# Other buffers for the weights of a second matrix product, and more for its left sides

## The chip, the cores and the metric

The kernel runs on one core of a Trainium2 chip. Its engines are TensorE (PE in the rows: matmuls, with its weight loads as PEld), VectorE (DVE), ScalarE (ACT), GpSimd (POOL) and SyncE (SP), which issues nearly all DMA transfers here. Each engine carries out its own list of instructions in order; so does SyncE, and a transfer that has to wait for a buffer holds up every transfer behind it in that list. The metric is the time of one execution in microseconds of device time, less is better. The time of a kernel is the median of several runs.

## The reference

One layer of a transformer-like block on x of 1024 x 1024 float32: a mixer (sparse attention and a gated delta rule), then an MLP of 4096 hidden columns with a squared ReLU. The change is in the MLP's second product.

```python
x = x + rms_norm(mix, post_norm_mix[l])
h = rms_norm(x, pre_norm_mlp[l])
y = jnp.square(jax.nn.relu(h @ w_mlp_in[l])) @ w_mlp_out[l]
x = x + rms_norm(y, post_norm_mlp[l])
```

## The kernel before, in words

A float32 matrix product is made of three matmuls at TensorE's fast 32-bit format (`mm3`, lines 199 to 201): each operand is split by `parts` into a rounded high part (a ScalarE cast, line 1422) and the rest (a VectorE subtraction, line 1423).

The hidden columns are 32 blocks of 128. Four of them (`NS`, "plain") are multiplied in the ordinary way. The other 28 go as 14 pairs i = 0 to 13 (`NP2`) through a scheme of Strassen's kind with 7 products j = 1 to 7 instead of 8; its left sides are sums of quarters of the hidden activations, its right sides sums of quarters of the weights. In the first product the seven combinations of each pair's hidden values are made by VectorE and ScalarE (lines 1593 to 1620) and written to DRAM (`spill`, lines 1560 to 1566: tensors `hid`). The second product takes the pairs in chunks, (0, 1), then (2, 3, 4) to (11, 12, 13), and in each chunk the products in the order j = 1, 2, 5, 3, 6, 7, 4. For each (chunk, j), `both_parts` loads the left sides: for j = 1, 2, 4 they lie in DRAM in two parts already and come straight into `hq` (`hl` for the first ones, line 1656), for the other j they come as one block into a `tmp` buffer (line 1659) and are split. The right sides come from `raw`, the 256 x 1024 block of w_mlp_out of pair i (1 MB, `raw_out`, line 1645); for some j a VectorE sum into `tt` stands in between (lines 1665 to 1677). TensorE adds up four banks per j, and VectorE takes each bank into `acc` or `acc_u` (`gather`: a copy the first time, line 1707; an addition after that, line 1704), after which the bank is free for a later j. The first banks that are taken so are those of j = 1 of the first chunk, and j = 2 adds on in the same banks.

At the end come the plain rows: `plain` is loaded into `stg` and split into `hq` (lines 1734 to 1736), their rows of w_mlp_out are loaded (line 1738) and split, and for each of the 8 row blocks `tb` TensorE computes two banks (`sc`, `ch`), VectorE adds them to `acc` (line 1763), and `finish` makes the norm, loads x (line 1745) into one of the two `stg` buffers, updates it (line 1751) and stores it (line 1753).

Buffers are rings: the pool `raw` (2 buffers of 8 KB a partition) is that of w_mlp_in in the first product and takes i = 0 and 1 after it; `raw2` (5 of 8 KB) takes i from 2 on; `hq` has 12 of 2 KB, `tmp2` 17 of 2 KB, `stg` 2 of 4 KB. The pools `hq`, `raw2` and `tt` open in `room()`, when the right sides of the first product are done with. A scheduler orders all instructions ahead of time for each engine from the program, so the order in which transfers stand in SyncE's list is not that of the source.

Of the kernel before, what the change touches and what calls it, by code (L numbers as in the profile page):

```python
# [8 lines left out]
F32 = mybir.dt.float32  # L9
F32R = mybir.dt.float32r  # L10
# [8 lines left out]
P = 128  # L19
T = 1024  # L20
D = 1024
# [118 lines left out]
def block_kernel(ctx: ExitStack, tc: tile.TileContext, x, w_in, c_norm, w_uk, w_uv, rel_bias, conv_w, a_log,  # L140
                 dt_bias, o_norm, w_out, pre_norm_mix, post_norm_mix, pre_norm_mlp, post_norm_mlp,
                 w_mlp_in, w_mlp_out, out, dbg=None):
    nc = tc.nc
    dbg = dbg or {}
    V, S, G, PE, SY = nc.vector, nc.scalar, nc.gpsimd, nc.tensor, nc.sync
    pl = Pools(tc)
# [4 lines left out]
    dt_bias, o_norm, w_out, w_mlp_in, w_mlp_out = dt_bias[0], o_norm[0], w_out[0], w_mlp_in[0], w_mlp_out[0]  # L151
# [12 lines left out]
    const, _ = pl.open("const")  # L164
    ps_t, _ = pl.open("ps_t", bufs=2, space=PSUM)
    ps_c, _ = pl.open("ps_c", bufs=2, space=PSUM)
    ps_w, ps_w_close = pl.open("ps_w", bufs=2, space=PSUM)
    dram, _ = pl.open("dram", space=DRAM)
# [82 lines left out]
    stg, stg_close = pl.open("stg", bufs=2)  # L251
# [56 lines left out]
    for tb in range(NB):  # L308
        xt = pl.t(px, [P, D], F32, f"x{tb}")
        r0 = tb // 4 * 512 + tb % 2 * 256 + tb % 4 // 2  # L310
# [13 lines left out]
    for half in range(2):  # L324
# [9 lines left out]
        for k in range(NK):  # L334
# [3 lines left out]
            sl = slice(half * 512, half * 512 + 512)  # L338
# [686 lines left out]
    ps_a, _ = pl.open("ps_a", bufs=2, space=PSUM)  # L1025
    ps_s, _ = pl.open("ps_s", bufs=2, space=PSUM)
# [221 lines left out]
    pool, wo, h2, early = {}, [], {}, []  # L1248
# [168 lines left out]
    def parts(src, eng, pool=None, tag="hl"):  # L1417

        hi = pl.t(pool or hlp, [P, 512], F32R, tag)
        lo = pl.t(pool or hlp, [P, 512], F32R, tag)  # L1420
        h_, l_ = (t.rearrange("p (a b) -> p a b", a=src.shape[1]) if len(src.shape) == 3 else t for t in (hi, lo))
        S.copy(h_, src)  # L1422
        eng.tensor_sub(l_, src, h_.bitcast(F32))  # L1423
        return hi, lo
# [35 lines left out]
    def tmp(dtype=F32):  # L1460
        return pl.t(tmpp, [P, 512], dtype, "tmp2")
# [168 lines left out]
    def room():  # L1630

        if rooms:
            return
        tq_close()
        h2_close()
        rooms["acc"], _ = pl.open("yacc")
        rooms["hq"], _ = pl.open("hq", bufs=12)
        rooms["raw"], _ = pl.open("raw2", bufs=5)
        rooms["tt"], _ = pl.open("tt", bufs=6)

    def raw_out(i, pool):

        raw = pl.t(pool, [P, 2, D], F32, "raw")
        r0 = (NS + 2 * i) * P
        SY.dma_start(raw, w_mlp_out[r0:r0 + 256, :].rearrange("(a p) d -> p a d", p=P))
        return raw

    def both_parts(c, j, raws, ts):

        res = []  # L1650
        for i in chunks[c]:
            own = (hlp, "hl") if c == 0 and j == 1 else (rooms["hq"], "hq")
            if WHICH[j] < 3:
                h = tuple(pl.t(own[0], [P, 512], F32R, own[1]) for _ in range(2))
                for a in range(2):
                    SY.dma_start(h[a].bitcast(F32), hid_d[i, WHICH[j]][:, a])
            else:
                f = tmp()
                SY.dma_start(f, hid_d[i, WHICH[j]])
                h = parts(f, V, *own)  # L1660
            raw = raws[i]
            b11, b12, b21, b22 = raw[:, 0, LO], raw[:, 0, HI], raw[:, 1, LO], raw[:, 1, HI]
            if j == 5:
                t = ts[i] = pl.t(rooms["tt"], [P, 512], F32, "tt")
                V.tensor_sub(t, b12, b11)
            elif j == 6:
                t = ts[i]
                V.tensor_sub(t, b22, t)
            elif j == 4:
                t = ts[i]  # L1670
                V.tensor_sub(t, b21, t)
            elif j == 7:
                t = pl.t(rooms["tt"], [P, 512], F32, "tt")
                V.tensor_sub(t, b22, b12)
            else:
                t = {1: b11, 2: b21, 3: b22}[j]
            res.append((h, parts(t, V)))
        return res

    def sides():  # L1680
        raws, ts = {}, {}
        for i in chunks[0]:
            raws[i] = raw_out(i, rawp)
        for c, ch in enumerate(chunks):
            for j in ORDER:
                if j in (3, 6) and c + 1 < len(chunks):
                    i = chunks[c + 1][(3, 6).index(j)]
                    raws[i] = raw_out(i, rooms["raw"])
                if (c, j) == (0, 2):
                    room()  # L1690
                yield c, j, both_parts(c, j, raws, ts)
            if c + 1 < len(chunks):
                raws[chunks[c + 1][2]] = raw_out(chunks[c + 1][2], rooms["raw"])

    gen = sides()
    ready = [next(gen)]
# [32 lines left out]
    fin, _ = pl.open("fin")  # L1729
    rows = []  # L1730
    for f in range(NS):
        hq = pl.t(rooms["raw"], [P, 2, T], F32R, "raw")
        r = pl.t(stg, [P, T], F32, "stg")
        SY.dma_start(r, plain_d[f])
        S.copy(hq[:, 0], r)
        V.tensor_sub(hq[:, 1], r, hq[:, 0].bitcast(F32))
        raw = pl.t(rawp, [P, D], F32, "raw")
        SY.dma_start(raw, w_mlp_out[f * P:(f + 1) * P, :])
        rows.append((hq, [parts(raw[:, sl], V, *((hlp, "hl") if f < 2 else (rooms["hq"], "hq"))) for sl in (LO, HI)]))
    def finish(tb, yt):  # L1740
        xr = pl.t(stg, [P, D], F32, "stg")

# [50 lines left out]
```

## Time and profile before

| | us |
|---|---|
| median of 3 runs | 1416.54 |
| fastest and slowest of them | 1414.64, 1420.17 |
| the profiled execution, its time | 1417.32 |
| its span, first to last instruction | 1415.6 |
| busy in it: PE, DVE, ACT, POOL | 1299.8, 1104.6, 730.1, 272.0 |

The rows further on come from the one profiled execution; their times count from the span's start. Its mean granted TensorE clock is 0.950 of full speed. The second MLP product's first transfers start near 1059 us, the plain rows' part near 1355 us. Matmuls overlap, so a matmul's row can be longer than its step: the step is read from the starts of successive rows, or from the count in a stretch that is busy throughout.

### The profile page before, as it was taken

Reading aid. Unit: us, or ns where it says so; the run is one execution under the profiler, and the core shown is the slowest. Engines: PE = TensorE matmul, PEld = TensorE weight load, DVE = VectorE, ACT = ScalarE, POOL = GpSimd, SP = SyncE. Lnnn points to the kernel's source line nnn. Section 1 sums busy time; section 2 is a strip of 40 time slices with the busy share of each in tenths; the row PEclk is TensorE's granted clock in tenths of the full one; section 3 lists DMA queues with packets and bytes.
Section 4 is the critical chain, followed back from the end, with each engine's and each line's share of the span. In section 5 each row is a group of like instructions: output and inputs, shape, how many; then the busy total and the mean of one; then the engine's idle time right before and its main releaser. Section 6 shows DMA issues by size and latency. Waiting matters only on the chain. (4 is left out here: it accounts for less than half of the span.)

```text
span 1415.6 us, 20269 instructions
## 1 busy us (share of the span) xinstructions
PE 1299.8 (92%) x6643; PEld 1120.9 (79%) x6643; DVE 1104.6 (78%) x2551; ACT 730.1 (52%) x1521; POOL 272.0 (19%) x296
## 2 busy tenths in 40 slices
PE   7898997998885999999999899999998799999995
PEld 4687894776675899997888688888887688888884
DVE  5524668999999798888768468878876887978975
ACT  5433436777651677677546456566565233333422
POOL 3154221121205335327420000000000000000023
PEclk8899998999995899999999899999999899999998
DMA  6133112456225433333556825555557956645224
GB/s 191 57 85 82 30 46 60 119 157 156 60 72 138 133 95 93 100 116 114 173 163 201 271 101 208 209 208 201 199 200 256 400 173 237 216 141 194 66 79 169
DMA packets 182931, 211.24 MB, mean 149 GB/s; under 512 B 28001, under 2 KB 123434, under 8 KB 182698
## 3 DMA queue, kind: packets, MB, share of 16 engines
q1 hardware_dynamic: 182826, 209.94, 46.3%
q8 instruction: 53, 0.87, 0.3%
q14 instruction: 52, 0.43, 0.1%
HBM read 136.48 MB, written 74.99 MB: 149 GB/s over the span
## 5 line engine op out<-in xcount | busy, mean ns | idle before, releaser
L199 PE MATMUL two<-hTH,wh 128*128 128x512 f32 (+1 forms) x416 | 166.8, 403 | 26.8 <-ACT tmp L424 16.0
L200 PE MATMUL two<-hTL,wh 128*128 128x512 f32 (+1 forms) x416 | 167.0, 401 | 0.0
L201 PE MATMUL two<-hTH,wl 128*128 128x512 f32 (+1 forms) x416 | 165.6, 398 | 0.0
L1750 POOL TENSOR_TENSOR tmp<-acc,c_row 128x512 f32<-128x512 f32 x16 | 20.7, 1302 | 644.3 <-DVE acc L1763 635.3
L199 PEld LDWEIGHTS two<-hTH,wh 128*128 128x128 f32 (+1 forms) x416 | 82.3, 198 | 44.4 <-issue 25.3
L521 ACT ACTIVATE jk<-score,cand 128x1024 bf16<-128x1024 f32 (+2 forms) x96 | 92.5, 966 | 46.0 <-DVE cand L532 29.4
L201 PEld LDWEIGHTS two<-hTH,wl 128*128 128x128 f32 (+1 forms) x416 | 82.1, 197 | 13.0 <-issue 0.8
L200 PEld LDWEIGHTS two<-hTL,wh 128*128 128x128 f32 (+1 forms) x416 | 82.5, 198 | 12.2 <-issue 0.5
L1422 ACT CAST hl<-raw 128x512 fp32r<-128x512 f32 x88 | 52.5, 614 | 53.6 <-PE acc L200 42.8
L1422 ACT CAST hq<-tmp 128x512 fp32r<-128x512 f32 x56 | 34.4, 616 | 79.5 <-PE tr L200 39.0
L270 POOL TENSOR_TENSOR wl<-stg,wh 128x1024 fp32r<-128x1024 f32 (+1 forms) x26 | 60.8, 2341 | 54.1 <-ACT wh L267 52.6
L1423 DVE TENSOR_TENSOR hl<-raw,hl 128x512 fp32r<-128x512 f32 x88 | 59.6, 685 | 7.3 <-ACT hl L1422 7.1
L1158 ACT ACTIVATE big<-big,nm 128x256 f32<-128x256 f32 (+6 forms) x64 | 50.6, 791 | 13.0 <-DVE nm L1157 13.0
L269 POOL TENSOR_SCALAR wh<-stg 128x1024 fp32r<-128x1024 f32 x19 | 19.9, 1048 | 194.0 <-PE two L200 194.0
L1422 ACT CAST hl<-tmp 128x512 fp32r<-128x512 f32 x56 | 33.3, 617 | 44.6 <-DVE tmp L1539 30.3
L1183 ACT CAST part<-tr 128x512 fp32r<-128x512 f32 x80 | 43.2, 543 | 20.3 <-PE tr L1181 16.6
L1184 DVE TENSOR_TENSOR part<-tr,part 128x512 fp32r<-128x512 f32 x80 | 50.2, 630 | 4.4 <-ACT part L1183 4.0
L1206 PE MATMUL acc<-part,VS 128*128 128x256 f32 x288 | 49.4, 295 | 1.3 <-DVE part L1184 1.0
L1422 ACT CAST hl<-tt 128x512 fp32r<-128x512 f32 x56 | 34.5, 615 | 31.1 <-PE tr L200 16.5
L1134 POOL TENSOR_TENSOR mt<-tz,maskb 128x256 f32<-128x256 f32 x56 | 38.5, 692 | 60.2 <-DVE mx L1150 39.6
L199 PE MATMUL sc<-hl,hq 128*128 128x512 f32 x112 | 42.7, 390 | 7.4 <-ACT hq L1422 7.4
L587 DVE SCALAR_TENSOR_TENSOR tmp<-two,svT,tmp 128x1023 f32<-128x1023 f32 (+2 forms) x36 | 45.5, 1275 | 4.0 <-ACT tmp L585 2.9
(514 smaller groups left out, 4161.5 us busy)
## 6 DMA issues: line engine op xcount, KB each, us to landing
hid<-tmp SPq DMA_DIRECT2D x140, 256.0 KB, 2.3
hq<-hid SPq DMA_DIRECT2D x80, 256.0 KB, 4.8
raw<-in_w_mlp_in_dram SPq DMA_DIRECT2D x14, 1024.0 KB, 5.6
raw<-in_w_mlp_out_dram SPq DMA_DIRECT2D x14, 1024.0 KB, 6.8
tmp<-hid SPq DMA_DIRECT2D x56, 256.0 KB, 5.2
stg<-in_w_in_dram SPq DMA_DIRECT2D x25, 512.0 KB, 4.2
x<-in_x_dram SPq DMA_DIRECT2D x8, 512.0 KB, 5.4
la_d<-la SPq DMA_DIRECT2D x8, 512.0 KB, 3.7
```

The costliest lines, as they stand in the source:

```text
L199: PE.matmul(o, lh, rh, start=start, stop=False, skip_group_check=more)
L200: PE.matmul(o, lh, rl, start=False, stop=False, skip_group_check=more)
L201: PE.matmul(o, ll, rh, start=False, stop=stop, skip_group_check=more)
L270: G.tensor_sub(wl[:, :, :n], f[:, :, :n], wh[:, :, :n].bitcast(F32))
L521: S.activation(junk[:, :n], s_of(b), AF.Sign, bias=cand[:, 3 + i:4 + i].bitcast(F32), scale=-1.0, accum_out=cnt[:, 3 + i:4 + i])
L587: V.scalar_tensor_tensor(acc[:, 3 - j:T], both[:, 0:T - 3 + j], w[j], acc[:, 3 - j:T], op0=OP.mult, op1=OP.add)
L1158: S.activation(pr[:, :n], pr[:, :n], AF.Exp, bias=nm, accum_out=den[:, hh:hh + 1])
L1183: S.copy(pt[:, 0:2 * nj, 0, :], v4(ps)[:, 0:2 * nj])
L1184: V.tensor_sub(pt[:, 0:2 * nj, 1, :], v4(ps)[:, 0:2 * nj], pt[:, 0:2 * nj, 0, :].bitcast(F32))
L1206: PE.matmul(po[:, hh * 256:hh * 256 + 256], VS[:, j + a, 2 * p + hh, :], pt[:, 2 * a + hh].rearrange("p a t -> p (a t)"), start=j + a + hh ...
L1422: S.copy(h_, src)
L1423: eng.tensor_sub(l_, src, h_.bitcast(F32))
```

## The change

`hq` gets 20 buffers instead of 12, and `raw2` 3 instead of 5: the same bytes. `raw_out` chooses the place by i: pair 0 takes two loads of 512 KB into the two `stg` buffers, pairs with i % 5 < 2 (1, 5, 6, 10, 11) the two buffers of the old ring `raw`, the others `raw2`. Of the plain rows' left sides three stay in `raw2` and the fourth goes into the old ring; their rows of w_mlp_out, four loads of 512 KB before, become eight of 256 KB into `tmp2` buffers. In all there are 5 more transfers. What is computed stays the same.

```diff
-        rooms["hq"], _ = pl.open("hq", bufs=12)
-        rooms["raw"], _ = pl.open("raw2", bufs=5)
+        rooms["hq"], _ = pl.open("hq", bufs=20)
+        rooms["raw"], _ = pl.open("raw2", bufs=3)
...
-    def raw_out(i, pool):
-
-        raw = pl.t(pool, [P, 2, D], F32, "raw")
+    def raw_out(i):
+
+
         r0 = (NS + 2 * i) * P
+        if i == 0:
+            raw = [pl.t(stg, [P, D], F32, "stg") for _ in range(2)]
+            for a in range(2):
+                SY.dma_start(raw[a], w_mlp_out[r0 + a * P:r0 + a * P + P, :])
+            return raw
+        raw = pl.t(rawp if i % 5 < 2 else rooms["raw"], [P, 2, D], F32, "raw")
         SY.dma_start(raw, w_mlp_out[r0:r0 + 256, :].rearrange("(a p) d -> p a d", p=P))
-        return raw
+        return [raw[:, 0], raw[:, 1]]
...
-        hq = pl.t(rooms["raw"], [P, 2, T], F32R, "raw")
+        hq = pl.t(rooms["raw"] if f < 3 else rawp, [P, 2, T], F32R, "raw")
...
-        raw = pl.t(rawp, [P, D], F32, "raw")
-        SY.dma_start(raw, w_mlp_out[f * P:(f + 1) * P, :])
-        rows.append((hq, [parts(raw[:, sl], V, *((hlp, "hl") if f < 2 else (rooms["hq"], "hq"))) for sl in (LO, HI)]))
+        w = []
+        for sl in (LO, HI):
+            raw = tmp()
+            SY.dma_start(raw, w_mlp_out[f * P:(f + 1) * P, sl])
+            w.append(parts(raw, V, *((hlp, "hl") if f < 2 else (rooms["hq"], "hq"))))
+        rows.append((hq, w))
```

SyncE's list at the change from the first product to the second. Before, hq loads (j = 2's left sides) stand ahead of the last pair's spills, and five loads of 1 MB stand ahead of the first tmp loads, those of j = 5:

```order
L1656 DMA hq_11214<-hid_1_1986_8446 128x512
L1656 DMA hq_11215<-hid_1_1986_8446 128x512
L1656 DMA hq_11222<-hid_1_1989_8449 128x512
L1656 DMA hq_11223<-hid_1_1989_8449 128x512
L1560 DMA hid_4_1982_8442<-tmp_2510_11139 128x512
...
L1645 DMA raw_11316<-in_w_mlp_out_dram 128x2x1024
L1566 DMA hid_2_2026_8486<-tmp_2504_11086 128x512
L1645 DMA raw_11371<-in_w_mlp_out_dram 128x2x1024
L1645 DMA raw_11530<-in_w_mlp_out_dram 128x2x1024
L1645 DMA raw_11729<-in_w_mlp_out_dram 128x2x1024
L1645 DMA raw_11805<-in_w_mlp_out_dram 128x2x1024
L1659 DMA tmp_2539_11263<-hid_4_1930_8390 128x512
```

The same place after the change:

```order
L1560 DMA hid_6_1984_8444<-tmp_2509_11135 128x512
L1566 DMA hid_0_2024_8484<-tmp_2507_11104 128x512
L1662 DMA hq_11216<-hid_1_1986_8446 128x512
L1662 DMA hq_11217<-hid_1_1986_8446 128x512
L1662 DMA hq_11224<-hid_1_1989_8449 128x512
L1662 DMA hq_11225<-hid_1_1989_8449 128x512
L1651 DMA raw_11318<-in_w_mlp_out_dram 128x2x1024
L1665 DMA tmp_2540_11265<-hid_4_1930_8390 128x512
L1665 DMA tmp_2546_11277<-hid_4_1934_8394 128x512
```

The hq loads have moved behind the spills, and one load of 1 MB instead of five stands between them and the tmp loads of j = 5.

VectorE at the same place, before: `raw_11182` is the block of pair 1, and the copies into acc_u free the first banks.

```order
L1600 TENSOR_TENSOR tmp_2509_11135<-sc_11054,tmp_2496_11046 128x512
L1423 TENSOR_TENSOR hl_11197<-raw_11182,hl_11196 128x512
L1423 TENSOR_TENSOR hl_11219<-raw_11180,hl_11218 128x512
L1604 TENSOR_TENSOR tmp_2510_11139<-tmp_2509_11135,tmp_2504_11086 128x512
...
L1674 TENSOR_TENSOR tt_11442<-raw_11182 128x512
L1564 TENSOR_TENSOR tmp_2507_11104<-tmp_2507_11104,tmp_2513_11152 128x512
L1707 COPY acc_u_11240<-ch_11230 128x512
```

VectorE after the change; `stg_11181` belongs to pair 0, `raw_11184` is pair 1:

```order
L1423 TENSOR_TENSOR hl_11199<-raw_11184,hl_11198 128x512
L1600 TENSOR_TENSOR tmp_2509_11135<-sc_11054,tmp_2496_11046 128x512
L1423 TENSOR_TENSOR hl_11221<-stg_11181,hl_11220 128x512
L1604 TENSOR_TENSOR tmp_2510_11139<-tmp_2509_11135,tmp_2504_11086 128x512
...
L1680 TENSOR_TENSOR tt_11444<-raw_11184 128x512
L1713 COPY acc_u_11242<-ch_11232 128x512
```

Pair 1's first subtraction has moved ahead of the addition of line 1600, and one instruction fewer stands between that addition and the first copy.

TensorE where the plain rows begin, before: `sc_13678` and `ch_13692` are the two banks of the first row block, `sc_13734` and `ch_13748` those of the second, and `raw_13663` is the fourth plain row.

```order
L201 MATMUL ch_13748<-hl_13629,raw_13618 128x512
L199 MATMUL ch_13748<-hl_13644,raw_13633 128x512
L199 MATMUL sc_13678<-hq_13670,raw_13663 128x512
L199 MATMUL sc_13734<-hq_13670,raw_13663 128x512
L200 MATMUL ch_13748<-hl_13645,raw_13633 128x512
L201 MATMUL ch_13748<-hl_13644,raw_13633 128x512
L200 MATMUL sc_13678<-hq_13671,raw_13663 128x512
L201 MATMUL sc_13678<-hq_13670,raw_13663 128x512
```

After the change the first row block's first bank is `sc_13688`, the second's `sc_13744`:

```order
L199 MATMUL sc_13688<-hq_13661,raw_13654 128x512
L200 MATMUL sc_13688<-hq_13662,raw_13654 128x512
L201 MATMUL sc_13688<-hq_13661,raw_13654 128x512
L199 MATMUL sc_13688<-hq_13678,raw_13671 128x512
L200 MATMUL sc_13688<-hq_13679,raw_13671 128x512
L201 MATMUL sc_13688<-hq_13678,raw_13671 128x512
L199 MATMUL sc_13744<-hl_13627,raw_13620 128x512
```

The last matmul of the first bank is row 5592 of TensorE's list before and row 5573 after; that of the same row block's second bank is row 5595 before and row 5588 after. The list is equally long.

## Rows read from the trace of the kernel before

**Rows 1.** Busy time of each engine by stretch: us, PE, PEld, DVE, ACT, POOL, clock, DMA share, GB/s.

```profile
1100.00:1150.00 50.00, 42.63 (x185) 36.54 (x184) 41.48 (x68) 16.06 (x28) 0.00 (x0) 0.90 0.89 333
1105.00:1110.00 5.00, 0.00 (x0) 0.00 (x0) 3.34 (x6) 0.58 (x1) 0.00 (x0) 0.56 1.03 401
1300.00:1350.00 50.00, 50.00 (x233) 43.80 (x232) 44.52 (x72) 20.44 (x35) 0.00 (x0) 1.00 0.26 85
```

**Rows 2.** TensorE's waits, 1075 to 1130: us in total, times, longest.

```profile
PE sc L199 <- ACT hq L1422: 7.4, 1, 7.4
PE ch L199 <- ACT hl L1422: 5.9, 1, 5.9
```

**Rows 3.** Timeline of TensorE: start, us, what, idle time before it and its releaser.

```profile
1095.83 0.77 PE L199 MATMUL ch<-hl,hq 128*128 128x512 f32 x1 [5.89 <-ACT hl L1422]
...
1098.89 0.38 PE L200 MATMUL ch<-hl,hq 128*128 128x512 f32 x1
...
1110.09 0.80 PE L199 MATMUL sc<-hl,hq 128*128 128x512 f32 x1 [7.37 <-ACT hq L1422]
...
1116.06 0.38 PE L201 MATMUL acc<-hl,hq 128*128 128x512 f32 x1
```

**Rows 4.** Timeline of VectorE at the change of products.

```profile
1086.78 0.69 DVE L1423 TENSOR_TENSOR hl<-raw,hl 128x512 fp32r<-128x512 f32 x1 [3.87 <-ACT hl L1422]
1087.83 0.69 DVE L1423 TENSOR_TENSOR hl<-raw,hl 128x512 fp32r<-128x512 f32 x1 [0.35 <-ACT hl L1422]
...
1095.05 1.28 DVE L1707 COPY acc_u<-ch 128x512 f32<-128x512 f32 x2
```

**Rows 5.** Timeline of ScalarE, at the change of products and before the end.

```profile
1086.13 0.62 ACT L1422 CAST hl<-raw 128x512 fp32r<-128x512 f32 x1 [4.49 <-DMA raw<-in_w_mlp_out_dram]
...
1360.15 1.14 ACT L1422 CAST hq<-raw 128x512 fp32r<-128x512 f32 x2 [3.70 <-DMA raw<-in_w_mlp_out_dram]
```

**Rows 6.** Timeline of SyncE's queue at the change of products.

```profile
1059.66 0.38 SPq L1645 DMA_DIRECT2D raw<-in_w_mlp_out_dram  x1
...
1078.12 0.38 SPq L1645 DMA_DIRECT2D raw<-in_w_mlp_out_dram  x1
...
1081.99 1.79 SPq L1656 DMA_DIRECT2D hq<-hid  x4
...
1090.53 1.00 SPq L1560 DMA_DIRECT2D hid<-tmp  x2
...
1093.00 2.50 SPq L1645 DMA_DIRECT2D raw<-in_w_mlp_out_dram  x4
1095.55 1.33 SPq L1659 DMA_DIRECT2D tmp<-hid  x2
```

**Rows 7.** The chain that ended last, 1085 to 1140: start, us, what.

```profile
1095.55 13.85 DMA tmp<-hid
```

**Rows 8.** Timeline of TensorE, its last matmul.

```profile
1397.72 0.38 PE L201 MATMUL ch<-hq,raw 128*128 128x512 f32 x1
```

**Rows 9.** Timeline of VectorE, from the first update to the last addition.

```profile
1370.99 1.42 DVE L1751 SCALAR_TENSOR_TENSOR stg<-tmp,rm_y,stg 128x512 f32<-128x512 f32 x2
...
1393.68 1.41 DVE L1751 SCALAR_TENSOR_TENSOR stg<-tmp,rm_y,stg 128x512 f32<-128x512 f32 x2 [2.13 <-DMA stg<-x_d]
...
1406.44 0.68 DVE L1763 TENSOR_TENSOR acc<-acc,ch 128x512 f32<-128x512 f32 x1
```

**Rows 10.** DMA issues, 1075 to 1145: count, KB each, median us to landing.

```profile
raw<-in_w_mlp_out_dram SPq DMA_DIRECT2D x6, 1024.0 KB, 9.9
hq<-hid SPq DMA_DIRECT2D x20, 256.0 KB, 5.4
```

**Rows 11.** DMA issues, 1350 to the end.

```profile
out_dram<-stg SPq DMA_DIRECT2D x32, 128.0 KB, 2.1
stg<-x_d SPq DMA_DIRECT2D x12, 256.0 KB, 3.1
```

**Rows 12.** A stretch of the first product, columns as in rows 1.

```profile
805.40:808.00 2.60, 1.22 (x2) 0.50 (x2) 0.00 (x0) 0.00 (x0) 0.00 (x0) 0.50 0.77 227
```

More of the change, by code (lines that the diff above doesn't have):

```diff
@@ L1661, in both_parts @@
             raw = raws[i]
-            b11, b12, b21, b22 = raw[:, 0, LO], raw[:, 0, HI], raw[:, 1, LO], raw[:, 1, HI]
+            b11, b12, b21, b22 = raw[0][:, LO], raw[0][:, HI], raw[1][:, LO], raw[1][:, HI]
             if j == 5:
@@ L1682, in sides @@
         for i in chunks[0]:
-            raws[i] = raw_out(i, rawp)
+            raws[i] = raw_out(i)
         for c, ch in enumerate(chunks):
@@ L1687, in sides @@
                     i = chunks[c + 1][(3, 6).index(j)]
-                    raws[i] = raw_out(i, rooms["raw"])
+                    raws[i] = raw_out(i)
                 if (c, j) == (0, 2):
@@ L1692, in sides @@
             if c + 1 < len(chunks):
-                raws[chunks[c + 1][2]] = raw_out(chunks[c + 1][2], rooms["raw"])
+                raws[chunks[c + 1][2]] = raw_out(chunks[c + 1][2])
     gen = sides()
```

## The prediction

> **What bounds the kernel now.** I read four views, each to answer one question: where TensorE stands still, what it stands behind, whether that is a transfer or an engine, and whether the end of the program is TensorE's at all.
>
> First the table by stretches [rows 1]. From 1300 to 1350 TensorE is busy all 50 us: in the second MLP product nothing else bounds. From 1100 to 1150 it lacks 7.4 of 50 us, at a granted clock of 0.90; in its worst 5 us TensorE does nothing at all while the DMA engines move 401 GB/s. The list of waits [rows 2] gives the two holes of that neighbourhood, 5.9 and 7.4 us; behind 1130 it lists no wait of TensorE. Each hole is followed by matmuls at the lower of the two clock levels [rows 3]: 7 steps from 1095.83 to 1098.89 take 3.06 us and 14 steps from 1110.09 to 1116.06 take 5.97, against 50 / 233 = 0.215 us a step at full clock [rows 1], so 1.56 and 2.97 us are lost on top. The change of products costs 5.9 + 7.4 + 1.56 + 2.97 = 17.8 us.
>
> Then what each hole waits for. The list names a ScalarE cast for the first, but that cast was long done; on VectorE the copy that frees the first bank starts at 1095.05 [rows 4], and 1095.83 follows its first half (0.60 us). The copy is late because VectorE stood 3.87 and 0.35 us at 1086.78 and 1087.83 behind casts of w_mlp_out. ScalarE waited there for the transfer itself, 4.49 us [rows 5]: that load, i = 1's, was issued only at 1078.12 [rows 6], when a buffer of the old ring came free, 18.5 us behind i = 0's. The second hole: four of the five 1 MB loads of the next pairs were issued in a row from 1093.00, the tmp<-hid loads that j = 5 needs came behind them at 1095.55 [rows 6], and the chain shows 13.85 us in that transfer [rows 7] until ScalarE can cast what it brought, at 1109.40.
>
> Last the end. TensorE's last matmul starts at 1397.72 and takes 0.38 [rows 8], so it ends at 1398.10. VectorE does its last addition only at 1406.44 [rows 9]: in between it goes round a loop over two buffers, store, load of x, update, with 2.13 us of waiting for x at 1393.68 alone. From 1406.44 to the end are 9.2 us; were that addition tied to TensorE, the kernel would end at 1398.1 + 9.2 = 1407.3, 8.3 us sooner.
>
> **The change, part by part.** All sums are against the profiled execution, 1417.32 us with a span of 1415.6; the median of the runs shown is 1416.54, so what I add up is taken off 1416.54 in the end.
>
> *A, the change of products.* i = 0's weights are loaded far ahead; i = 1's take the queue's place of 1059.66 and land before ScalarE reaches them, also if they take the 9.9 us of the median there [rows 10]. So the 3.87 and 0.35 us on VectorE go; its row of the copy also has one instruction fewer ahead of it (0.60). The copy comes 3.87 + 0.35 + 0.6 = 4.8 us earlier, at 1090.25, and its first half ends at 1090.9. But the four loads of j = 2's left sides, issued at 1081.99 before, now stand behind the last pair's spills and wait for their order. These spills began 4.2 us earlier than their old 1090.53 [rows 6] end at about 1087.3, so the loads go out from 1087.8; the first pair takes about 4.2 us to land (between half and all of the 5.4 us that these 256 KB loads have as median in this stretch [rows 10]), and TensorE goes on at about 1092.0: 2.0 us of the 5.9 stay. j = 2 has 24 steps, 5.2 us, and 1.56 more at the lower level, which I leave in the sum: to 1098.7. j = 5's tmp loads go out at about 1091, behind one 1 MB load instead of five; with 5.4 us, a cast (0.62) and a subtraction (0.69) they are ready at 1097.7, or at 1099.7 if VectorE's queue costs 2 us, so I leave 1.0 us of the 7.4 and, against myself, the whole 2.97 of the lower level. Left: 2.0 + 1.56 + 1.0 + 2.97 = 7.5; **gain 10.3 us**. Bounds: 4.8 if only the copy's head start counts, because VectorE, which has work without a gap behind the copy, hands TensorE everything in turn; 16.6 if nothing is left but 1.2 us for the copy of the bank itself.
>
> No byte is moved that was not moved before, and the DMA engines are full there, so the 1 MB loads taken out of the way are owed later; from 1150 on nothing waits for them, since TensorE has no wait there [rows 1, 2].
>
> Here a rule speaks against the change. The measured fact is 401 GB/s in a stretch of mostly 256 KB loads [rows 1, 10]. The Trainium skill ("DMA: Bandwidth & Descriptors", section "Rules for kernel authors") asks for at least 1 MiB a DMA for the full bandwidth, and this change splits a 1 MB load in two and four of 512 KB in eight. By that rule the split ones would move more slowly and add some microseconds to the queue; by the trace they lose nothing that can be seen, and the sum has no term for it.
>
> *B, the end.* The plain rows' weights now arrive in halves in tmp buffers, early, where before the last two came into the ring of the old weights, the last cast pair only at 1360.15 after 3.70 us of waiting [rows 5]. TensorE's own order changes with it: the first row block's first bank is complete 19 matmuls earlier (4.1 us at 0.215) and its second bank 7 earlier (1.5). The first update, at 1370.99 [rows 9], needs both, so it comes between 1.5 and 4.1 us earlier; I take the middle, 2.8. From there to the end were 1415.6 - 1370.99 = 44.6 us. I followed the eight row blocks through the new order of the queue with the stores' 2.1 and the x loads' 3.1 us to landing [rows 11], 0.6 an issue and 1.41 an update [rows 9]: one x load half now goes out ahead of the second block's stores, and the loop comes to 42.0, 2.6 less. **Gain 5.4 us**; bounds 8.3 (TensorE's end) and -1.6 (one more landing of 3.1 in the loop, less the 1.5).
>
> *C, around 800 us.* The two 512 KB loads of i = 0 go into the buffers that the plain rows used. One stands ahead of the loads that the turning of h waits for, at a moment when TensorE has just lost its clock (0.50 from 805.4, [rows 12]). At the 401 GB/s of [rows 1] it takes 1.3 us; VectorE's order takes one subtraction (0.6) out of the way there: **0.7 us lost**, bounds 0 and 1.5.
>
> *Free parts.* Pools change places in equal bytes. The eight more hq buffers only let loads go out earlier. The five more DMAs are some 0.6 us of issuing each on SyncE; TensorE, busy all of 1300 to 1350 [rows 1], hides them, and without that cover they would cost 3 us. The new waits (a plain row's load into the two-buffer ring, and i = 6's weights behind it, both on late VectorE work of the first chunk, with j = 4's left sides queued behind them) fall about 15 us before TensorE needs what stands behind.
>
> Sum: -10.3 - 5.4 + 0.7 = -15.0 us, 1417.3 to 1402.3; on the median's side **1401.5**.
>
> **Rivals.**
> *R1, VectorE takes the second hole back.* With the first hole closed VectorE, 44.5 of 50 us busy later on [rows 1], is the one that TensorE waits for, and the clock falls again. Then A is 4.8: -4.8 - 5.4 + 0.7 = -9.5, 1407.0.
> *R2, the end gives nothing.* The two-buffer loop is the same loop, and starting it sooner only makes it wait longer. Then -10.3 + 0.7 = -9.6, 1406.9. Against it: the first update's place is set by TensorE's order, which moved.
> *R1 and R2 together*: -4.8 + 0.7 = -4.1, 1412.4, no change that can be told. That the change doesn't do what it says has no case of its own: the places in the queue did move.
> *R3, slower.* Pairs from 2 on have three new buffers and two old ones in place of five. Should the old two come free late, each of the three later chunk borders would wait for a 1 MB load: 9.9 us to land [rows 10], thrice, -15.0 + 29.7 = +14.7, 1431. It decides where the last reader of a buffer ends less than 9.9 + 0.62 + 0.69 = 11.2 us before TensorE's first matmul with the next weights. Against it: the cycle is still five long, each load waits for the pair five before it, as it did, and those loads have no wait of TensorE behind them now [rows 1, 2]. The Trainium skill ("Perfetto Trace Analysis", section "Identifying Performance Opportunities") says that the same gap coming again and again can mean too few buffers; no such row is in the trace of before, and only this rival would make one.
>
> **How the numbers follow.** Forecast 0.60 (its own range 1396 to 1406), R1 0.12, R2 0.15, both 0.08, R3 0.05. Forecast, R1 and R2 lie within 1395 to 1411, the low end being A near 14 with B at 8; about 0.15 is left out. A change of 0.5%, 7 us, is about what a measurement of this kernel can tell: faster than 1409.5 are the forecast and most of R1 and R2, 0.85; within, 0.10; slower, R3, 0.05.
>
> **What the profile after would show.** A: SyncE loads only one 1 MB block ahead of j = 5's loads; the VectorE copies into acc_u start near 1090; TensorE's waits between 1085 and 1130 sum to 3 to 5 us instead of 13.3. B: the first update near 1358, and 42 us from it to the end. C: the half-clock stretch near 805 about a microsecond later. I am wrong if the holes of 1090 to 1116 come back under another name (VectorE, as in R1), if the last 45 us keep their length, or if gaps appear at the chunk borders near 1160, 1220 and 1280.

## The result, and the profile after

| | before | changed |
|---|---|---|
| median of 22 runs each, us | 1417.22 | 1409.69 |
| ratio, 95% interval | | 0.9949 [0.9936, 0.9961] |
| profiled execution: span, us | 1415.6 | 1409.4 |
| mean granted clock | 0.950 | 0.955 |

The change gains 7.2 us (0.51% of 1417.2; 5.5 to 9.1 by the interval). One of the 22 executions of the changed kernel took 2665.6 us, and the ratio is taken without it. Forecast were 15.0, so the direction was right and the size less than half of it.

Two executions differ by some microseconds long before the change has any instruction. So stages are compared: the table of the experiments counts from the start of one TensorE matmul to that of another with the same place in the list. The stage "products" runs from the 5251st to the 5551st matmul row, the first chunk's change of products: 1079.21 to 1162.03 before (82.8 us), 1081.43 to 1158.44 after (77.0); without any wait 300 steps of 0.2158 us take 64.7. Behind it TensorE never waits, in either: from the 5551st to the last, the 6643rd, both need 235.7 us. From the last matmul's start to the end are 17.9 us before and 15.2 after. So 5.8 us came from the change of products, 2.7 from the end, and 0.6 from the stretch ahead of both, the first product from the 3901st to the 5251st matmul (302.5 and 301.8 us), 9.1 in all. The changed kernel's execution was 2.84 us late at the 3901st matmul, before any of it, which leaves the 6.2 between the spans.

Two stretches after the change, the first of them one of [rows 1] (us, PE, PEld, DVE, ACT, POOL, clock, DMA share, GB/s):

```profile
1105.00:1110.00 5.00, 4.97 (x23) 4.38 (x24) 5.00 (x9) 2.92 (x6) 0.00 (x0) 1.00 1.05 403
1120.00:1130.00 10.00, 6.83 (x27) 5.63 (x28) 9.60 (x17) 2.18 (x4) 0.00 (x0) 0.91 1.04 396
```

From 1105 to 1110, where TensorE had stood still, it is busy throughout, while the DMA engines carry as much as before, 403 GB/s. Ten microseconds later it stands again. From 1075 to 1140 the two holes of [rows 2], 13.3 us, have become five of 9.5. TensorE's timeline shows them in order, each with its length and what ended it, and answers to [rows 3]:

```profile
1095.52 0.45 PE L199 MATMUL ch<-hl,hq 128*128 128x512 f32 x1 [3.35 <-DMA hq<-hid]
...
1102.11 0.48 PE L199 MATMUL sc<-hl,hq 128*128 128x512 f32 x1 [1.17 <-ACT hq L1422]
...
1105.03 0.48 PE L201 MATMUL sc<-hl,hq 128*128 128x512 f32 x1 [0.93 <-DVE hq L1423]
...
1120.75 0.45 PE L199 MATMUL sc<-hl,hq 128*128 128x512 f32 x1 [1.63 <-DVE acc L1713]
...
1128.59 0.77 PE L199 MATMUL sc<-hl,hq 128*128 128x512 f32 x1 [2.43 <-DMA hq<-hid]
```

The first stands ahead of j = 2, the next two within j = 5, the fourth ahead of j = 7, the last ahead of j = 4. Only behind the last do the matmuls run at the lower clock (a row of 0.77 us instead of 0.45; the granted clock is 0.50 from 1128.59 to 1131.60). VectorE's first copy stands at 1092.88. This execution is 2.2 us later at the 5251st matmul, so on the clock of before that is 1090.7. The copy that ended the fourth hole stands at 1119.89:

```profile
1092.88 0.69 DVE L1713 COPY acc_u<-ch 128x512 f32<-128x512 f32 x1
...
1119.89 0.71 DVE L1713 COPY acc<-sc 128x512 f32<-128x512 f32 x1
```

Between the two VectorE has no wait at all. TensorE had finished j = 6's two `sc` banks by 1116.5, more than 3 us before the second copy, so this hole is VectorE's: the copy waited only for its turn in VectorE's list.

SyncE's queue shows what the last hole waited for; it answers to [rows 6]:

```profile
1091.13 2.22 SPq L1662 DMA_DIRECT2D hq<-hid  x4
1093.39 0.43 SPq L1651 DMA_DIRECT2D raw<-in_w_mlp_out_dram  x1
1093.87 1.19 SPq L1665 DMA_DIRECT2D tmp<-hid  x2
...
1113.16 0.32 SPq L1740 DMA_DIRECT2D stg<-plain  x1
1113.88 3.75 SPq L1665 DMA_DIRECT2D tmp<-hid  x4
1117.96 0.32 SPq L1740 DMA_DIRECT2D stg<-plain  x1
1118.64 0.38 SPq L1651 DMA_DIRECT2D raw<-in_w_mlp_out_dram  x1
1119.27 0.32 SPq L1665 DMA_DIRECT2D tmp<-hid  x1
1120.62 9.59 SPq L1662 DMA_DIRECT2D hq<-hid  x11
```

The first of those eleven hq loads are j = 4's. They went out from 1120.62 on, 5.5 us before TensorE wanted them (1128.59 - 2.43), behind two plain rows, one 1 MB load and the tmp loads of the second chunk, in a stretch in which the DMA engines are full. Four views belong to the end: the second update before (the first, at 1370.99, is in [rows 9]); after the change the first three updates, SyncE's queue among them, and TensorE's last matmul:

```profile
1373.60 2.13 DVE L1751 SCALAR_TENSOR_TENSOR stg<-tmp,rm_y,stg 128x512 f32<-128x512 f32 x2 [0.46 <-DVE rm_y L217]
```

```profile
1364.62 2.29 DVE L1760 SCALAR_TENSOR_TENSOR stg<-tmp,rm_y,stg 128x512 f32<-128x512 f32 x2
...
1369.57 1.42 DVE L1760 SCALAR_TENSOR_TENSOR stg<-tmp,rm_y,stg 128x512 f32<-128x512 f32 x2
...
1376.65 1.42 DVE L1760 SCALAR_TENSOR_TENSOR stg<-tmp,rm_y,stg 128x512 f32<-128x512 f32 x2 [1.28 <-issue]
```

```profile
1370.31 0.48 SPq L1754 DMA_DIRECT2D stg<-x_d  x1
1370.88 2.50 SPq L1762 DMA_DIRECT2D out_dram<-stg  x4
1373.42 2.60 SPq L1754 DMA_DIRECT2D stg<-x_d  x3
```

```profile
1394.13 0.38 PE L201 MATMUL ch<-hq,raw 128*128 128x512 f32 x1
```

Set against TensorE's end (1398.10 before, 1394.51 after), the first update came 2.8 us sooner (27.1 us ahead of it before, 29.9 after), the second only 0.4 (24.5 and 24.9).

### The profile page after: what moved, and what is told of

Read it like the earlier page. It is cut to its first block, busy times and chain, and to the rows that moved or that the text cites. A ratio compares the mean times of both kernels' runs of the same rounds, so it can differ in the third digit from the quotient of the medians.

```text
span 1409.4 us, 20293 instructions
## 1 busy us (share of the span) xinstructions
PE 1298.3 (92%) x6643; PEld 1119.7 (79%) x6643; DVE 1104.0 (78%) x2551; ACT 729.7 (52%) x1521; POOL 271.1 (19%) x296
## 4 chain that ended last, share of the span: by engine, by line
PE 66%; DVE 19%; DMA 6%; ACT 5%; issue 2%; SPq 1%; DVEq 0%; ACTq 0%
PE ch L201 4%; PE sc L199 4%; PE acc L200 4%; PE acc L199 4%; PE sc L201 4%; PE sc L200 4%; PE ch L199 4%; PE acc L201 4%; PE ch L200 4%; PE two L199 4%; PE two L200 4%; PE two L201 4%; DVE pre L527 2%; PE tr L199 2%; PE tr L200 2%
## 5 line engine op out<-in xcount | busy, mean ns | idle before, releaser
L200 PEld LDWEIGHTS two<-hTL,wh 128*128 128x128 f32 (+1 forms) x416 | 81.9, 197 | 12.3 <-issue 0.7
L1422 ACT CAST hl<-raw 128x512 fp32r<-128x512 f32 x81 | 48.5, 614 | 72.9 <-PE acc L200 48.0
L1423 DVE TENSOR_TENSOR hl<-raw,hl 128x512 fp32r<-128x512 f32 x81 | 55.7, 692 | 6.3 <-PE acc L201 3.4
L1158 ACT ACTIVATE big<-big,nm 128x256 f32<-128x256 f32 (+6 forms) x64 | 50.6, 791 | 13.5 <-DVE nm L1157 13.5
L201 PE MATMUL ch<-h2H,hl 128*128 128x512 f32 x112 | 43.6, 390 | 3.6 <-DVE hl L1423 3.6
```

The costliest lines, as they stand in the source:

```text
L200: PE.matmul(o, lh, rl, start=False, stop=False, skip_group_check=more)
L201: PE.matmul(o, ll, rh, start=False, stop=stop, skip_group_check=more)
L1158: S.activation(pr[:, :n], pr[:, :n], AF.Exp, bias=nm, accum_out=den[:, hh:hh + 1])
```

## The experiments

Ratios are to the kernel before, with 95% intervals. "Products" is the stage of 300 matmuls, "last" the time from the last matmul's start to the end, "second" that from the second update to the end; they come from one profiled execution each.

| | ratio | products | last | second |
|---|---|---|---|---|
| before | 1 | 82.8 | 17.9 | 42.0 |
| changed | 0.9949 [0.9936, 0.9961] | 77.0 | 15.2 | 39.8 |
| changed, again (e9) | 0.9951 [0.9927, 0.9976] | 75.0 | 15.3 | 39.8 |
| e1, halves alone | 0.9996 [0.9973, 1.0019] | 82.1 | 16.8 | 41.7 |
| e2, without halves | 0.9971 [0.9949, 0.9993] | 74.7 | 20.2 | 42.5 |
| e3, 12 hq | 0.9954 [0.9932, 0.9976] | 76.7 | 16.7 | 41.7 |
| e4, pair 0 in the old ring | 0.9964 [0.9944, 0.9985] | 80.2 | 15.8 | 40.4 |
| e5, no loads of pairs 2 to 13 | 0.9931 [0.9904, 0.9959] | 72.4 | 13.9 | 38.9 |
| e6, subtractions on GpSimd | 0.9950 [0.9919, 0.9981] | 76.0 | 15.8 | 40.1 |
| e7, x in tt | 0.9930 [0.9898, 0.9963] | 75.6 | 12.2 | 36.8 |
| e8, 24 hq, 13 tmp | 0.9936 [0.9905, 0.9968] | 73.2 | 13.5 | 38.9 |
| e10, x in tt, 24 and 13 | 0.9945 [0.9925, 0.9965] | 73.3 | 11.3 | 36.7 |
| e11, x in tt, 22 and 15 | 0.9915 [0.9886, 0.9945] | 73.5 | 12.3 | 36.8 |
| e12, e11 and plain rows in tmp | 0.9907 [0.9874, 0.9940] | 73.0 | 14.1 | 39.0 |

The intervals are some 0.2 to 0.3% wide to either side, 3 to 4 us, so single edits are judged by the stages. In the stage "products" four executions have the same matmuls and the same transfers in the same order: the two of the changed kernel, and those of e2 and e7, which edit the end alone. They take 77.0, 75.0, 74.7 and 75.6 us, so a difference of less than 2.3 us between two single executions says nothing there.

**e9, the changed kernel again.** No edit.

> The changed kernel itself a second time, beside the others on one chip: how far the 300 matmuls of the change of products (77.0 us in its profile; 74.7 in a kernel with the same list of transfers there) and the 44.7 us from the first update to the end differ between executions of one list. Expected: 74.5 to 77.5 us, 44 to 46 us, ratio 0.994 to 0.996.

As expected, ratio and stages. Its waits stand at the same matmuls as those of the first execution, the first 2.6 and the last 1.9 us long:

```profile
PE ch L199 <- DVE acc_u L1713: 2.6, 1, 2.6
PE sc L199 <- DMA hq<-hid: 1.9, 1, 1.9
PE sc L199 <- DVE acc L1713: 1.6, 1, 1.6
PE sc L201 <- DVE hq L1423: 1.3, 1, 1.3
PE sc L199 <- ACT hq L1422: 1.1, 1, 1.1
```

No matmul of the stage runs at half clock here (granted clock 1.00 from 1090 to 1135). For the first hole the list names VectorE's copy here and the hq load in the first execution; the two ended within 0.2 us of each other in both, so the name decides nothing.

**e1, the halves alone, on the kernel before.**

```diff
-        raw = pl.t(rawp, [P, D], F32, "raw")
-        SY.dma_start(raw, w_mlp_out[f * P:(f + 1) * P, :])
-        rows.append((hq, [parts(raw[:, sl], V, ...
+        for sl in (LO, HI):
+            raw = tmp()
+            SY.dma_start(raw, w_mlp_out[f * P:(f + 1) * P, sl])
+            w.append(parts(raw, V, ...
```

> The kernel before with one part of the change alone: the plain rows' w_mlp_out comes in eight 256 KB halves through tmp buffers instead of four 512 KB loads through the old ring. The profile after shows the first update 2.8 us earlier against TensorE's last matmul (1370.99 to 1364.62, TensorE's end 1398.10 to 1394.51) and the time from that update to the end unchanged (44.6 and 44.8). Theory 1: the halves cause that head start, so this kernel gains about 2.7 us, ratio 0.998, and the change of products keeps its holes of 5.9 and 7.4 us. Rival: the head start comes from the order of the x loads, which the stg buffers changed, and the halves alone give nothing, ratio 1.000.

The first update does come sooner against TensorE's end, 30.2 us ahead of it instead of 27.1. But the second is 25.2 ahead instead of 24.5, and 1.1 us are left of it at the end (17.9 to 16.8). The ratio cannot tell that from nothing. Theory 1 named the cause and not the size.

**e2, the changed kernel without the halves** (the same lines, the other way).

> The changed kernel with that one part undone: the plain rows' w_mlp_out in four 512 KB loads through the old ring. Theory 1: the gain up to TensorE's last matmul stays (holes between 1085 and 1130 of 3.4, 1.2, 0.9, 1.6, 2.4 us) and the 2.6 us behind it go, ratio about 0.9968. Rival: the halves matter nothing, ratio as the changed kernel's, 0.9949; or the old ring, of which one buffer now holds the fourth plain row, makes the loads wait for each other, and TensorE stands some microseconds at the plain rows, ratio 0.998 to 1.000.

The gain up to the last matmul stays (74.7), and the end takes 20.2 us instead of 15.2: 5 us, so the halves carry all of the gain at the end and more. ScalarE shows why whole rows in the old ring are late:

```profile
1342.67 1.14 ACT L1422 CAST hq<-raw 128x512 fp32r<-128x512 f32 x2 [3.78 <-DMA raw<-in_w_mlp_out_dram]
...
1349.95 1.14 ACT L1422 CAST hq<-raw 128x512 fp32r<-128x512 f32 x2 [3.64 <-DMA raw<-in_w_mlp_out_dram]
```

It waits for the third and the fourth row, as in [rows 5].

**e3, 12 hq buffers.**

```diff
-        rooms["hq"], _ = pl.open("hq", bufs=20)
+        rooms["hq"], _ = pl.open("hq", bufs=12)
```

> The changed kernel with 12 hq buffers instead of 20; all else stays. The order of SyncE's list then has j = 2's hq loads ahead of the last pair's spills again, and three 1 MB loads and one of 512 KB in a row ahead of j = 5's tmp loads. Theory 1 (with the DMA engines full at some 400 GB/s, the order of the queue decides what TensorE waits for): the first hole shrinks to 1 to 2 us, the second comes back with 3.5 MB at 400 GB/s = 8.8 us of transfers ahead of it, 4 to 6 us and a stretch at half clock behind it; ratio about 0.997 to 0.998. Rival (VectorE, which is busy without a gap behind 1092, hands TensorE everything late whatever the queue does): no difference from the changed kernel, 0.995.

```profile
PE sc L199 <- ACT hq L1422: 8.0, 1, 8.0
PE ch L199 <- ACT tmp L1563: 1.5, 1, 1.5
```

The two holes are where theory 1 put them, the second longer than the 4 to 6 us that it said. Three 1 MB loads and a plain row stand ahead of j = 5's tmp loads, as expected:

```profile
1093.18 1.83 SPq L1651 DMA_DIRECT2D raw<-in_w_mlp_out_dram  x3
1095.11 1.00 SPq L1740 DMA_DIRECT2D stg<-plain  x1
1096.15 1.30 SPq L1665 DMA_DIRECT2D tmp<-hid  x2
```

But the stage takes 76.7 us, as long as with 20 buffers: what is loaded ahead of j = 5 is missing from the queue later, and no hole follows behind. Theory 1 had the place right and the sum wrong. The eight more hq buffers, and with them the interleaving of 1 MB and tmp loads, give nothing that these runs can tell; they spread one hole over four.

**e4, pair 0 in the old ring.**

```diff
-        if i == 0:
-            raw = [pl.t(stg, [P, D], F32, "stg") for _ in range(2)]
-            ...
-            return raw
```

> The changed kernel with pair 0's weights in the old ring again, so that pair 1's load is issued near 1080 as before; hq, raw2 and the end stay as changed, and 1 MB loads and tmp loads stay interleaved. Theory 1: the first hole comes back, ScalarE and VectorE waiting for pair 1's load some 4 us, TensorE 5 to 6 us with a half-clock stretch behind, while no hole of 7 us follows; ratio about 0.997. Rival (VectorE's later backlog decides how far TensorE gets, so the early load only shifts the wait): ratio as the changed kernel's, 0.995.

```profile
PE ch L199 <- DVE acc_u L1708: 4.6, 1, 4.6
PE sc L199 <- DVE hl L1423: 3.7, 1, 3.7
```

ScalarE waits 3.24 us for pair 1's load again, TensorE 4.6 us for the copy behind it, with half clock after it, and the stage takes 80.2 us: 3 to 5 more than the changed kernel's 77.0 and 75.0. The first hole and its half clock come back as theory 1 has it, so the early load of pair 1 carries 3 to 5 of the 6 to 8 us gained at the change of products. Not all of that is the first hole: the second line is the hole ahead of j = 4, 1.3 to 1.8 us longer than in the changed kernel and followed by half clock too, and why it grew was not tried.

**e5, no loads of pairs 2 to 13.**

```diff
-                    raws[i] = raw_out(i)
+                    raws[i] = raws[1]
...
-                raws[chunks[c + 1][2]] = raw_out(chunks[c + 1][2])
+                raws[chunks[c + 1][2]] = raws[1]
```

> The changed kernel without the 1 MB loads of pairs 2 to 13: these pairs take pair 1's weights instead, so 12 MB of transfers are left out and the output is not the reference's; no instruction of TensorE, VectorE or ScalarE is left out. Between 1090 and 1130 some 4 MB, 10 us at 400 GB/s, go out of the queue. Theory 1 (the DMA engines, full there, bound what is left of the change of products): the holes from 1100 on, 1.2, 0.9, 1.6 and 2.4 us with 1.7 us of half clock behind, mostly go, and from the last matmul that both kernels have in the same place before to the 300th behind it take 70 to 72 us instead of 77.0 (before the change 82.8, with no wait 64.7). Rival (VectorE, without a gap from 1092 to 1129 in the changed kernel, is the bound): 75 to 77 us.

```profile
PE ch L199 <- DVE acc_u L1713: 3.3, 1, 3.3
PE sc L199 <- DVE acc L1713: 0.8, 1, 0.8
```

72.4 us: the holes at j = 5 and j = 4 are gone. VectorE is as busy from 1110 to 1130 as in the changed kernel (20.0 and 19.6 of 20 us), so that is the transfers' doing. The hole at j = 7 is halved, but not by the transfers: TensorE's list has four matmuls of another product there (4 x 0.2158 = 0.9 us), and without them the wait for VectorE's copy would be about 1.6 us again. What also stays is the first hole, behind VectorE's copy, with a half-clock stretch behind it.

**e6, the first chunk's left-side subtractions on GpSimd.**

```diff
-                h = parts(f, V, *own)
+                h = parts(f, G if c == 0 else V, *own)
```

> The changed kernel with the 8 VectorE subtractions that split the first chunk's tmp left sides moved to GpSimd, which has nothing to do there: 8 x 0.6 = 4.8 us less on VectorE, 1.3 us each on GpSimd. Theory 1 (transfers bound): those 300 matmuls take 76 to 78 us as before, or longer by the 0.6 us that a GpSimd subtraction takes more. Rival (VectorE bound): 73 to 75 us; the 1.6 us that TensorE waits for VectorE's copy near 1119 and the 0.9 near 1105 go.

76.0 us. The edit did not relieve VectorE. While GpSimd subtracts, VectorE's own sums and subtractions take up to 1.77 us instead of 0.7; its copies out of TensorE's banks stay at 0.68:

```profile
1102.39 12.88 POOL L1423 TENSOR_TENSOR hq<-tmp,hq 128x512 fp32r<-128x512 f32 x8 [357.50 <-ACT hq L1422]
```

```profile
1107.79 1.76 DVE L1423 TENSOR_TENSOR hl<-tt,hl 128x512 fp32r<-128x512 f32 x1
...
1111.14 0.68 DVE L1713 COPY acc<-sc 128x512 f32<-128x512 f32 x1
...
1117.54 0.68 DVE L1423 TENSOR_TENSOR hl<-tt,hl 128x512 fp32r<-128x512 f32 x1
```

Seven such instructions are 5.7 us longer together, more than the 4.8 us that were to be saved. TensorE's order changed as well: j = 6 begins earlier, a wait of 1.7 us for VectorE's copy stands ahead of it, and none ahead of j = 7. The first hole is 3.7 us, with a half-clock stretch behind it that neither execution of the changed kernel has; the other waits are 0.5, 0.4, 0.4 and 0.2. So this run is no test of VectorE as the bound and doesn't tell the theories apart.

**e8, 24 hq and 13 tmp buffers.**

```diff
-        rooms["hq"], _ = pl.open("hq", bufs=20)
+        rooms["hq"], _ = pl.open("hq", bufs=24)
...
-    tmpp, _ = pl.open("tmp2", bufs=17, side="right")
+    tmpp, _ = pl.open("tmp2", bufs=13, side="right")
```

> The changed kernel with 24 hq buffers and 13 tmp buffers instead of 20 and 17: the same bytes. In SyncE's list j = 4's hq loads of the first chunk now stand ahead of four tmp loads of the second chunk more, with no wait for TensorE; the first plain row's load goes ahead of the last spills. Theory 1: the hole of 2.4 us in front of j = 4 and the half clock behind it go, the 300 matmuls take 72 to 74 us instead of 77.0; fewer tmp buffers may cost a little in the first product. Rival (VectorE bound): TensorE comes to j = 4 no sooner, 76 to 78 us.

```profile
1112.86 0.39 SPq L1651 DMA_DIRECT2D raw<-in_w_mlp_out_dram  x1
1114.48 10.37 SPq L1662 DMA_DIRECT2D hq<-hid  x13
```

j = 4's loads go out at 1114.48 instead of 1120.62, and TensorE waits for no transfer ahead of j = 4: 73.2 us, as theory 1 expected. The hole there isn't gone, though. 1.3 us of it stay, which the list puts down to a ScalarE cast here and to VectorE's addition in e10, whose lists of matmuls and transfers in this stage are the same:

```profile
PE sc L199 <- ACT hl L1422: 1.3, 1, 1.3
```

Ahead of the stage the fewer tmp buffers cost: from the 3901st to the 5251st matmul 304.8 us, against 301.8 and 302.3 in the two executions of the changed kernel.

At the end this run shows something that its expectation does not ask about. Its x still goes through the two stg buffers, but its list puts four stores and two loads of x in turn:

```profile
1362.18 1.12 SPq L1754 DMA_DIRECT2D stg<-x_d  x2
1363.40 2.46 SPq L1762 DMA_DIRECT2D out_dram<-stg  x4
1367.51 1.12 SPq L1754 DMA_DIRECT2D stg<-x_d  x2
```

The updates then come 5.2 to 5.4 us apart up to the seventh, where the changed kernel has gaps of 7.1 and 7.2 us, and the end is 1.7 us shorter (13.5 instead of 15.2).

**e7, x in the tt buffers.**

```diff
-        xr = pl.t(stg, [P, D], F32, "stg")
+        xs = [pl.t(rooms["tt"], [P, 512], F32, "tt") for _ in range(2)]
...
-            V.scalar_tensor_tensor(xr[:, cs], yg, r, xr[:, cs], op0=OP.mult, op1=OP.add)
+            V.scalar_tensor_tensor(xs[c], yg, r, xs[c], op0=OP.mult, op1=OP.add)
```

> The changed kernel with the end's x loads and updates in the six 2 KB tt buffers (three row blocks in flight) instead of the two stg buffers, in 256 x 512 pieces. Theory 1, as in the prediction (the two-buffer loop of store, load, update bounds the end): the waits for x and for stores go, the time from the first update to the end falls from 44.7 to 39 or 40 us, ratio 0.991 to 0.992. Rival 2 (the chain of one row block bounds it: addition, ScalarE's squares, root, update, and the next block's addition behind that update in VectorE's list, 5.3 us a block in the last four blocks of the changed kernel): 43 to 45 us, ratio 0.994 to 0.995.

```profile
1361.26 2.28 DVE L1761 SCALAR_TENSOR_TENSOR tt<-tmp,rm_y,tt 128x512 f32<-128x512 f32 x2
...
1366.20 1.42 DVE L1761 SCALAR_TENSOR_TENSOR tt<-tmp,rm_y,tt 128x512 f32<-128x512 f32 x2
...
1371.51 1.42 DVE L1761 SCALAR_TENSOR_TENSOR tt<-tmp,rm_y,tt 128x512 f32<-128x512 f32 x2
```

From the first update to the end are 41.7 us instead of 44.7: between the two theories. The gap of 7.1 us between the second and the third update falls to 5.3, as it does in e8 with the two stg buffers. So two buffers alone do not force that gap; what goes with it is the order of stores and loads in the queue. The next four updates come 5.2 us apart with no wait for a transfer. TensorE's 24 matmuls of a block take 24 x 0.2158 = 5.2 us as well, but from 1362 to 1396 VectorE waits for none of TensorE's banks, only for ScalarE (5.5 us in 13 waits). So there the chain of one block bounds, which is rival 2's cause, with TensorE close behind.

**e10, e11, e12, edits together.** e10 is e7 and e8; e11 has 22 and 15 buffers; e12 has in addition

```diff
-        r = pl.t(stg, [P, T], F32, "stg")
-        SY.dma_start(r, plain_d[f])
+        for sl in (LO, HI):
+            r = tmp()
+            SY.dma_start(r, plain_d[f][:, sl])
```

> The changed kernel with both edits that shortened a stage: x in tt buffers, and 24 hq with 13 tmp buffers. If the two are independent, as theory 1 has it (the queue's order at the change of products, the two-buffer ring at the end): 300 matmuls in 73 to 74 us, first update to the end 41.5 to 42.5, and with about 1.4 us lost before 1066 to the fewer tmp buffers a ratio of 0.990 to 0.992. Rival (whatever the change of products gives is given back at the end): no better than either alone, 0.993 to 0.994.

> As the one with 24 and 13, with 22 hq and 15 tmp buffers: j = 4's hq loads still ahead of the second chunk's j = 6 tmp loads, two of them with a wait for TensorE, and two tmp buffers more for the first product. Theory 1: the hole in front of j = 4 below 1 us, 300 matmuls in 73 to 75 us, no 1.4 us lost in the first product; ratio 0.990 to 0.992.

> As the last one, with the plain rows' left sides in halves through tmp buffers as well, so that their two 512 KB loads (2.6 us at 400 GB/s) leave the full stretch of the queue. Theory 1: j = 4's loads go out 2 to 3 us sooner, and the 300 matmuls take 1 to 2 us less than with 22 buffers alone, 72 to 73.5. Rival (VectorE bound by then): the same within 0.5 us.

In e10 both stages come out as expected (73.3, 41.9 us from the first update to the end), and the ratio doesn't: from the 3901st to the 5251st matmul it takes 307.5 us, 5 more than the changed kernel, which eats the gain. Expected were 1.4 us for 13 tmp buffers. e8 shows 2.5 to 3.0 us for them, and e10 has the same additional waits; what goes beyond is more time at half clock (from 800 to 820 the granted clock is 0.74, in e8 0.83). With 15 (e11) that stretch takes 302.3, the stage 73.5 us, the hole ahead of j = 4 0.5 us:

```profile
PE sc L199 <- DVE acc L1710: 0.5, 1, 0.5
```

and the kernel's 1402.9 us are a ratio of 0.9915: it beats the kernel before clearly, and the changed one by its stages (1.5 to 3.5 us at the change of products, 3 at the end); the two ratios' intervals overlap a little. The four kernels with j = 4's loads further ahead, e8, e10, e11 and e12, take 73.0 to 73.5 us at the change of products, the four executions of the changed list 74.7 to 77.0. e12 has no hole ahead of j = 4 and 73.0 us, 0.5 less than e11. That is what the rival said, but it is too little to tell it from theory 1. Its end is 1.9 us longer than e11's, with the x loads at other places in the queue; why was not tried.

## Why the prediction was right or wrong

**A, the change of products: right in its mechanism, 10.3 us forecast, 5.8 and 7.8 measured** (77.0 and 75.0 against 82.8). The early load of pair 1 did what it was said to do: the two waits on VectorE are gone, and the copy stands at 1092.88 - 2.2 = 1090.7, forecast 1090.25. e4 shows that this edit carries more than half of the gain. Of the holes, the first was to keep 2.0 us and kept 3.4 and 2.6: j = 2's hq loads went out at 1091.13 - 2.2 = 1088.9, forecast 1087.8. The second was to keep 1.0 and kept 2.1 and 2.4 in two pieces. The 4.5 us of half clock left in the sum were too many: outside the holes 77.0 - 64.7 - 9.5 = 2.8 and 75.0 - 64.7 - 8.5 = 1.8 us were lost.

The step that failed is that nothing was counted behind j = 5. TensorE's waits were to sum to 3 to 5 us and sum to 9.5 and 8.5; the holes ahead of j = 7 and j = 4, 4.0 and 3.5 us of that, had no term. The free parts say that the new waits "fall about 15 us before TensorE needs what stands behind". They don't. j = 4's loads stood behind them and behind the second chunk's tmp loads, came 2.4 and 1.9 us late, and brought the lower clock in one of the two executions. And the "1 MB loads taken out of the way are owed later" were put at nothing, on the ground that TensorE had no wait behind 1130: but that ground was the trace of before, in which TensorE had stood still long enough for the queue to get ahead. Once it stands less, it needs the next loads sooner, at the same 400 GB/s. e5 measures that term: without the 4 MB the stage takes 72.4 us, 2.3 to 4.6 less than the four executions of the changed list. By another order of the queue e8, e10, e11 and e12 get 2.3 us on the average, 73.3 against 75.6, without a byte less.

**R1, that VectorE takes the second hole back**, was right in small. The 1.6 us ahead of j = 7 are VectorE's: it works without a pause up to that copy, and the same 1.6 us stand there in e9, e2, e7, e11 and e12. The 1.3 us that stay ahead of j = 4 in e8 and e10 wait for no transfer either, and in e2, with the lists of the changed kernel, the list names VectorE's addition for the 1.6 us there; that addition and j = 4's first load ended within 0.2 us of each other. Most of the rest the list puts down to transfers or to casts of what they brought, and e5 confirms it for j = 5 and j = 4. No run took work from VectorE: e6, which was to do it, made VectorE's other instructions longer by as much.

**B, the end: 5.4 forecast, 2.7 and 2.6 measured** (15.2 and 15.3 against 17.9). The head start of the first update was right, 2.8 us, but by luck: it was taken as the middle of 1.5 and 4.1, though the update needs both banks and the second was only 7 matmuls, 1.5 us, earlier. The other 1.3 us came behind that bank: VectorE's addition of the first bank was done 3.2 us ahead of the second's (1356.99 and 1360.23), where before both came in one go (1364.68 and 1365.33), and from the second addition to the update are 4.4 us instead of 5.7. The failed step is adding to this head start a loop that begins there. The second row block's second bank ends with the same matmul row, the 6499th, before and after, so the second update came only 0.4 us sooner and the head start was spent in a longer gap between the first and the second (4.9 us instead of 2.6). From the second update on, the loop is 2.2 us shorter (42.0 to 39.8), near the 2.6 of the forecast; 0.4 + 2.2 = 2.6 is the gain. The half load of x that goes out earlier gains nothing, since the third update needs both halves. The premise that the two-buffer loop bounds the end holds only for the gaps of 7.1 and 7.2 us and for this order of the queue: they vanish with more buffers (e7), and also with another order in the same two (e8).

**C, around 800 us: 0.7 forecast as a loss, 0.6 and 0.2 measured as a gain** (from the 3901st to the 5251st matmul 302.5 before, 301.8 and 302.3 after): nothing that can be told from no change.

**R2**, that the end gives nothing, is refuted by the two executions of the changed kernel (15.2 and 15.3 us instead of 17.9) and by e2 (20.2). Its mechanism is there in part: the second update gets 0.4 of the first one's 2.8 us. **R3**, waits at the chunk borders for want of buffers, did not come: 235.7 us from the 5551st to the last matmul, before and after, without a wait. The Trainium skill ("Perfetto Trace Analysis", section "Identifying Performance Opportunities") says that the same gap coming again and again can mean too few buffers; no such gap stands in this stretch. And the split loads cost nothing that shows at 403 GB/s; at the end they are the gain, by e2.

## What to carry to other kernels

While an engine stands still, the queue that feeds it gets ahead, so a trace with that pause cannot show which loads are late without it. Where the DMA engines are full, count for each later step the bytes queued ahead of its loads, from the new start, before its wait is put at nothing. And a head start for one block of a loop is worth what the next block also gets of it: follow the second round before adding the first one's gain to the loop's. Before an edit is taken as relief for an engine, look whether the engine's other instructions kept their length.

## What the runs showed of the hardware

TensorE's lower clock, a granted 0.50, did not follow each hole. In the changed kernel the hole of 3.4 us at 1095.52 had none behind it and that of 2.4 us at 1128.59 had; in the second execution of the same list neither had. Before, both holes had (5.9 and 7.4 us), and in e4 those of 4.6 and 3.7. The first hole was 2.8 us long in e2, e8 and e12: e8 had a granted clock of 0.50 behind it, e2 and e12 had 1.00. So a hole of a few microseconds cost between itself and itself with 3 us more, the loss behind the second one before [rows 3].

VectorE ran slower beside GpSimd in e6: while GpSimd's eight subtractions ran (1.27 to 1.74 us each), VectorE's sums and subtractions between buffers took up to 1.77 us instead of 0.7, and its copies out of TensorE's banks 0.68 as ever.
